# Decode attention and decode state reads as fp32 matmuls on four 32-column tiles, state loads on POOL's queue

## The chip, the core and the metric

The kernel runs on one core of one Trainium2 chip. TensorE (PE in the profile) multiplies, VectorE (DVE) and ScalarE (ACT) do elementwise work and empty PSUM, GpSimd (POOL) and SyncE (SP) issue transfers. The metric is the device time of one execution in microseconds.

## What is computed

The reference is one decoder layer for a prompt of 256 tokens and eight sequences that decode one token each. One input, two mixers in parallel, gates and an output projection:

```python
# A: sparse attention, 8 query heads on 2 key heads, head size 128
o_cmp, o_slc, o_win = nsa_sample(q, kv_cmp, kv_slc, kv_win, cache_cmp, cache_slc, st_win, page_table, cw, slopes)
#   slc: q @ kg, softmax, p @ vg over 15 gathered blocks of 64 keys and the new token, per sequence
#   win: the same over 511 keys of the window state and the new token; the state is shifted by one and stored
# B: gated delta rule, 8 heads, one 128 x 128 state per head and decoding sequence
#   o = S q, v_new = beta (v - S k), S = decay S + v_new k^T
```

The change concerns the decode side of `slc`, `win` and B. The prompt's attention and its chunked delta rule (which ends in a state `S` that is stored) lie beside it.

## The kernel before

Nearly all work of PE is the projections: 256 prompt tokens and 8 decode tokens are the 264 moving columns, and every weight tile of 128 by 1024 fp32 (512 KB, `raw`) is split into two fp32r halves, `hi` on ACT and `lo` on DVE, of which three products are accumulated in tile `acc`. Such a weight tile is 24 matmuls and is called a half here. There are 7536 `acc` matmuls.

Everything else is written as generators (`g_dec_slc`, `g_dec_win`, `g_attn`, `g_gdn`, `g_gdn_dec` and others) that advance by one `yield` per 12 `acc` matmuls (`tick`). A string `ORDER` sets which projection comes when. From what the generators emit, the Tile framework's scheduler makes a fixed order for PE, ACT and DVE; SP and POOL keep the order in which the code issues. Each engine takes its instructions strictly in that order. SP issues the weight loads; `raw`, `hi` and `lo` have three buffers each. Large tiles (`wk`, `gk`, `gv`, `sst` and their fp32r copies) share one pool of 13 slots through `slot`.

Decode attention. `gather` (L898) fetches 15 blocks for one sequence and both key heads: `gk` keys, `gv` values, two indirect transfers of POOL each, one sequence ahead. Keys are transposed by PE (`gtr`) and copied as fp32r pair into `gkx`. `qk` multiplies them by the query, which is a zero-padded fp32r pair `qm`: 128 rows hold `hi` and `lo` of all 64 query rows, so each sequence and key head adds into one PSUM tile (`gsc` for slc, `wsc` for win): per 480 or 512 keys one matmul of 128 columns and one of 64. `split1` (L801 on ACT, L802 on DVE) makes the pairs of the window keys (`wkx`), the values (`gvx`, `wvx`); `pt_split` transposes the probabilities (`ptr`) and splits them. `pv_part` multiplies them with the values (`pvo`, 256 columns), and `pv_take` (L797) adds the rows of one sequence to `acc2` on DVE. `smo` transposes `acc2` at the end.

Delta rule. `g_gdn` inverts the prompt's triangular matrices (`inv`, through `lanes`, `td`, `U` and `prod`, which go through memory on POOL's queue), then runs the chunks (`uw`, `dS`, `vn`, `og`), stores `S` with POOL's last transfer `o_S<-prod` (L1341) and transposes the output (`ogt`). `g_gdn_dec` takes the decode states two sequences at a time (1 MB, tile `sst`): load on SP (L1423), 16 fp32 matmuls that hold a head's state as weights and move 64 columns of `wq` (`sw`), three small DVE operations for `dvn` and `dod`, scaling of 16 state tiles by the decay on ACT (L1448), a rank-one update from a broadcast transpose (`vnb`, L1449) and a store on ACT's queue. `inv`, `uw`, `dS`, `vn`, `og`, `sw`, `vnb` run in PSUM tiles of one pool of two buffers. The gates Z of these outputs (`zt`, `oh`, `ol`) are projected in the same stretch; `zt` is the first reader that frees an `acc` tile there.

Of the kernel before, what the change touches and what calls it, by code (L numbers as in the profile page):

```python
# [10 lines left out]
F32 = mybir.dt.float32  # L11
# [37 lines left out]

def shape_constants():  # L50
# [12 lines left out]
    for t in range(2):  # L63
# [8 lines left out]
    row = np.arange(64)  # L72
    srow = slope[(row // 32) * 4 + row % 4]
    c.add("c64", srow[:, None] * np.arange(64)[None])
    c.add("wrow", srow[:, None] * (np.arange(8) * 64 - 512)[None])
    c.add("e64", (row[None] // 4) == np.arange(16)[:, None])
    c.add("sel", ((row[None, None] // 32) == np.arange(2)[None, :, None])
          & (((row[None, None] // 4) % 8) == np.arange(8)[:, None, None]))
    c.add("rmask", ((p[:, None] % 64) // 4) == np.arange(16)[None])
# [57 lines left out]
def program(tc, A):  # L137
# [94 lines left out]
    grow = cp.tile([64, 2], F32, name="grow")  # L232
# [260 lines left out]
    def g_qstat(h):  # L493
# [7 lines left out]
        if h == 7:  # L501
# [88 lines left out]
    def g_small(ps):  # L590
# [38 lines left out]
    def g_dec_cmp():  # L629
# [95 lines left out]
    def new_token(w):  # L725
        yield from wait("q")
        pr = tp.tile([128, 64], F32, name="ntp", tag="a", bufs=NA)
        V.tensor_tensor(pr.rearrange("p (g b r) -> p g b r", g=2, b=NB), qd,
                        knT[:, w, :, :, None].to_broadcast([128, 2, NB, 4]), ALU.mult)
        yield 3  # L730
        pt = psb("ntk")
        mm(pt[0:64, 128:129], pr, ones[:, 0:1])
        for g in range(2):
            mm(pt[0:64, 0:128], C("sel", 8)[:, 64 * g:64 * g + 64], L["kvd"][:, w, 1, g, :], start=g == 0, stop=g == 1)
        sn = tp.tile([64, 8], F32, name="ntm", tag=f"ntm{w}")
        ve = tp.tile([64, 128], F32, name="ntv", tag=f"ntv{w}")
        V.tensor_scalar(sn[:, 0:1], pt[0:64, 128:129], SCALE, None, ALU.mult)
        S.activation(ve, pt[0:64, 0:128], AF.Copy)
        L["nt", w] = sn, ve
        mark(("nt", w))  # L740

    def row_softmax(sc, n, w):
# [11 lines left out]
        V.scalar_tensor_tensor(acc2[0:64], ve, sn[:, 4:5], acc2[0:64], ALU.mult, ALU.add)  # L754

    def scores(out, sc, bias, shape):
        lo = slot("slo", [64, 960])
        lo = lo[:, 0:math.prod(shape)]
        for k, ps in enumerate(out):
            n = math.prod(shape) // len(out)  # L760
            S.activation(lo[:, n * k:n * k + n], ps[64:128, 0:n], AF.Copy, scale=SCALE)
            V.scalar_tensor_tensor(sc[:, n * k:n * k + n], ps[0:64, 0:n], SCALE, lo[:, n * k:n * k + n], ALU.mult, ALU.add)
        V.tensor_add(sc, sc, bias)
# [11 lines left out]
    def pt_split(name, sc, nt, np_):  # L775
        pt = psb("ptr")
        for t in range(nt):
            tr(pt[0:np_, 64 * t:64 * t + 64], sc[:, np_ * t:np_ * t + np_])
        P_ = slot(name, [128, 8, 128], F32R)
        v = pt[0:np_, 0:64 * nt].rearrange("p (t c) -> p t c", t=nt)  # L780
        S.activation(P_[0:np_, 0:nt, 0:64], v, AF.Copy)
        V.tensor_sub(P_[0:np_, 0:nt, 64:128], v, P_[0:np_, 0:nt, 0:64])
        return P_

    def pv_part(po, P_, np_, ts, nt, hi, lo):
        for t in ts:
            h = lambda: mm(po[:, 0:256], P_[0:np_, t, :], hi(t), start=t == 0, stop=t == nt - 1)
            if t == 0:
                h()
            mm(po[0:64, 0:256], P_[0:np_, t, 0:64], lo(t), start=False, stop=False)  # L790
            if t:
                h()

    def pv_take(po, b):
        for g in range(2):
            i = 8 * g + b
            V.scalar_tensor_tensor(acc2, po[:, 128 * g:128 * g + 128], C("rmask")[:, i:i + 1], acc2, ALU.mult, ALU.add)  # L797

    def split1(name, src, shape, np_=128):
        x = slot(name, [128, 2] + shape, F32R)  # L800
        S.activation(x[0:np_, 0], src, AF.Copy)  # L801
        V.tensor_sub(x[0:np_, 1], src, x[0:np_, 0])  # L802
        return x

    def g_dec_win():
# [30 lines left out]
        def wk_qk(b, x):  # L836
            for g in range(2):
                qk(ps, 8 * g + b, x[:, 0, g], x[:, 1, g], b + g == 0, b * g == 7)

        prev = None  # L840
        for b in range(NB):
            if b % 2 == 0:
                if b < 6:
                    load_k(b // 2 + 1)
                else:
                    load_v(0)
            x = split1("wkx", kr[b // 2][:, b % 2, :, 0:512], [2, 512])
            if prev is not None:
                yield 3
                wk_qk(b - 1, prev)  # L850
            prev = x
        yield 2
        wk_qk(7, prev)
        bb = slot("wb", [64, 2, 512])
        V.tensor_tensor(bb[:, 0].rearrange("p (n m) -> p n m", m=64), C("wrow", 64)[:, :, None].to_broadcast([64, 8, 64]),
                        C("c64", 64)[:, None, :].to_broadcast([64, 8, 64]), ALU.add)
        sc = bb[:, 1]
        yield 7
        scores([ps], sc, bb[:, 0], [512])
# [3 lines left out]
        P_ = pt_split("wP", sc, 4, 128)  # L863
        def wv_pv(b, x):
            po = PV("pvo")
            pv_part(po, P_, 128, range(4), 4, lambda t: x[:, 0, t], lambda t: x[:, 1, t])
            pv_take(po, b)

        prev = None
        for b in range(NB):  # L870
            if b % 2 == 0 and b < 6:
                load_v(b // 2 + 1)
            x = split1("wvx", vr[b // 2][:, b % 2], [4, 256])
            if prev is not None:
                yield
                wv_pv(b - 1, prev)
            prev = x
        yield 5
        wv_pv(7, prev)
        yield 7  # L880
        pt = psb("smo")
        yield 2
        for i in range(2):
            mm(pt[:, 0:64], acc2, ident[:, 64 * i:64 * i + 64], start=i == 0, stop=i == 1)
        V.tensor_add(oD, oD, pt[:, 0:64])
        mark("oD")

    def g_dec_slc():
        yield from wait("idx")
        yield from wait(("kv", 0), 4)  # L890
        G.memset(acc2, 0.0)
# [15 lines left out]
        def gk_qk(b, g, x):  # L907
            for half in range(2):
                o = slice(480 * half, 480 * half + 480)
                qk(ps[half], 8 * g + b, x[:, 0, o], x[:, 1, o], b + g == 0, b * g == 7)  # L910

        prev = None
        for b in range(NB):
            if b < NB - GP:
                kr[b + GP] = gather("gk", "cslk", b + GP)
            elif b - NB + GP < VP:
                vr[b - NB + GP] = gather("gv", "cslv", b - NB + GP)
            for g in range(2):
                x = slot("gkx", [128, 2, 960], F32R)
                for half in range(2):  # L920
                    pt = psb("gtr")
                    for t in range(4):
                        tr(pt[:, 120 * t:120 * t + 120], kr[b][0:120, g, 4 * half + t, :])
                    o = slice(480 * half, 480 * half + 480)
                    S.activation(x[:, 0, o], pt[:, 0:480], AF.Copy)
                    V.tensor_sub(x[:, 1, o], pt[:, 0:480], x[:, 0, o])
                    yield
                if prev:
                    gk_qk(*prev)
                prev = b, g, x  # L930
            del kr[b]
        yield 6
        gk_qk(*prev)
        bb = slot("sb", [64, 2, 960])
        V.tensor_tensor(bb[:, 0].rearrange("p (t n m) -> p t n m", t=8, n=15),
                        L["sbias"][:, None, 0:15, None].to_broadcast([64, 8, 15, 8]),
# [792 lines left out]
```

## Time and profile before

| | us |
|---|---|
| median of three runs | 1146.93 (1146.84 to 1148.42) |
| profiled execution | 1147.96 |
| its span in the trace | 1146.2 |
| PE busy | 1116.5 |
| PE loading weights (beside matmuls) | 1090.7 |
| DVE busy | 777.0 |
| ACT busy | 603.5 |
| POOL busy | 146.6 |

A matmul's row in the trace has a start and a modelled end; because matmuls are pipelined, rows overlap, and what one costs is the distance from its start to the next one's start. An fp32 matmul (not fp32r) has two rows. A granted clock of 1.00 is 2.4 GHz, 0.50 is 1.2 GHz.

### The profile page before, as it was taken

To read this page: it belongs to the slowest core of one execution; us is meant where nothing else is said; L and a number is where in the kernel's file an instruction comes from. 1 tells how busy PE (TensorE), PEld (TensorE's weight loads), DVE (VectorE), ACT (ScalarE), POOL (GpSimd) and SP (SyncE) were. 2 spreads that over 40 slices of the span, in tenths; PEclk is the share of its full clock that TensorE was granted. 3 is DMA by queue.
4 is the path that set the end of the run, shared out by engine and by line. 5 is a ranking of instruction groups with operands and counts; after the bars stand their busy time and mean duration, and the time that the engine had idled before them with its cause. 6 is when DMAs were issued, how large, how long until landed. Compare 5 with 4: busy or idle time off the path is not lost.

```text
span 1146.2 us, 24552 instructions
## 1 busy us (share of the span) xinstructions
PE 1116.5 (97%) x9088; PEld 1090.7 (95%) x9088; DVE 777.0 (68%) x1619; ACT 603.5 (53%) x1165; POOL 146.6 (13%) x218
## 2 busy tenths in 40 slices
PE   4999999999999999999899999999999999999998
PEld 4989999999999998998899999999999999999998
DVE  3587665444667886996888977699746685567543
ACT  4455655445635776785566644444344844454332
POOL 4430344200001311114110300100100000000000
PEclk9999999999999999999999999999999999999999
DMA  8874676335536775467996944655752555555673
GB/s 299 256 233 142 195 216 205 124 111 165 169 121 197 210 203 154 127 190 191 261 356 240 330 152 163 180 181 175 214 179 108 212 186 183 185 179 204 213 238 128
DMA packets 76842, 222.74 MB, mean 194 GB/s; under 512 B 10465, under 2 KB 27370, under 8 KB 75186
## 3 DMA queue, kind: packets, MB, share of 16 engines
q1 hardware_dynamic: 59922, 168.55, 45.5%
q0 software_dynamic: 14784, 45.61, 14.0%
q10 hardware_dynamic: 2016, 7.01, 1.6%
q8 instruction: 71, 1.16, 0.4%
q14 instruction: 49, 0.40, 0.1%
HBM read 203.14 MB, written 17.99 MB: 193 GB/s over the span
## 4 chain that ended last, share of the span: by engine, by line
PE 85%; DVE 4%; DMA 3%; issue 1%; ACT 1%; POOL 0%; ACTq 0%; POOLq 0%; DVEq 0%
PE acc L197 70%; DMA gv<-cslv,idx 2%; DVE lo L325 1%; PE po L197 1%; PE gsc L197 1%; PE gtr L194 1%; DVE lanes L1227 1%; PE ps L197 1%; PE sw L197 1%; DMA raw<-win 1%; PE inv L197 1%; PE cf L197 1%; DVE prod L1226 1%; PE pvo L197 1%; PE uw L197 1%
## 5 line engine op out<-in xcount | busy, mean ns | idle before, releaser
L324 ACT ACTIVATE hi<-raw 128x1024 fp32r<-128x1024 f32 (+1 forms) x250 | 264.1, 1056 | 328.4 <-PE acc L197 265.4
L197 PE MATMUL acc<-xh,hi 128*128 128x264 f32 (+1 forms) x1488 | 428.9, 288 | 0.3 <-ACT gate L1491 0.3
L197 PE MATMUL acc<-xl,hi 128*128 128x264 f32 (+1 forms) x1488 | 426.8, 287 | 0.0
L197 PE MATMUL acc<-xh,lo 128*128 128x264 f32 (+1 forms) x1488 | 425.6, 286 | 0.0
L325 DVE TENSOR_TENSOR lo<-raw,hi 128x1024 fp32r<-128x1024 f32 (+1 forms) x250 | 304.3, 1218 | 171.5 <-ACT hi L324 168.7
L197 PEld LDWEIGHTS acc<-xl,hi 128*128 128x128 f32 (+1 forms) x1488 | 280.6, 189 | 2.0 <-issue 0.6
L197 PEld LDWEIGHTS acc<-xh,hi 128*128 128x128 f32 (+1 forms) x1488 | 280.5, 189 | 2.0 <-ACT gate L1491 0.6
L197 PEld LDWEIGHTS acc<-xh,lo 128*128 128x128 f32 (+1 forms) x1488 | 279.6, 188 | 1.7 <-issue 0.5
L197 PE MATMUL acc<-hi,w1h 128*128 128x254 f32 (+1 forms) x512 | 147.7, 289 | 15.9 <-ACT hi L401 15.9
L197 PE MATMUL acc<-lo,w1h 128*128 128x254 f32 (+1 forms) x512 | 146.5, 286 | 3.3 <-DVE lo L402 3.1
L197 PE MATMUL acc<-hi,w1l 128*128 128x254 f32 (+1 forms) x512 | 145.1, 283 | 0.0
L402 DVE TENSOR_TENSOR lo<-rawc,hi 128x512 fp32r<-128x512 f32 (+2 forms) x136 | 84.1, 656 | 52.1 <-ACT hi L401 45.9
L197 PEld LDWEIGHTS acc<-hi,w1h 128*128 128x128 f32 x512 | 97.9, 191 | 16.0 <-ACT hi L401 15.9
L401 ACT ACTIVATE hi<-rawc 128x512 fp32r<-128x512 f32 (+2 forms) x136 | 74.7, 599 | 61.3 <-PE acc L197 56.5
L197 PEld LDWEIGHTS acc<-lo,w1h 128*128 128x128 f32 x512 | 98.6, 192 | 4.5 <-DVE lo L402 4.3
L197 PEld LDWEIGHTS acc<-hi,w1l 128*128 128x128 f32 x512 | 98.3, 192 | 0.1
L378 POOL DMA_DIRECT2D rawc<-ccmp x125 | 67.4, 539 | 97.7 <-issue 72.6
L197 PE MATMUL acc<-oh,hi 128*128 128x264 f32 x256 | 73.6, 287 | 0.2 <-ACT gate L1491 0.2
L197 PE MATMUL acc<-ol,hi 128*128 128x264 f32 x256 | 73.5, 287 | 0.0
L197 PE MATMUL acc<-oh,lo 128*128 128x264 f32 x256 | 73.4, 287 | 0.0
L197 PE MATMUL acc<-mh,hi 128*128 128x264 f32 x256 | 72.7, 284 | 0.0
L197 PE MATMUL acc<-ml,hi 128*128 128x264 f32 x256 | 72.6, 283 | 0.0
(453 smaller groups left out, 1651.9 us busy)
## 6 DMA issues: line engine op xcount, KB each, us to landing
raw<-win SPq DMA_DIRECT2D x184, 512.0 KB, 3.7
raw<-wpab SPq DMA_DIRECT2D x32, 512.0 KB, 3.3
raw<-wo SPq DMA_DIRECT2D x32, 512.0 KB, 3.5
rawc<-ccmp SPq DMA_DIRECT2D x126, 128.0 KB, 3.1
rawc<-ccmp POOLq DMA_DIRECT2D x125, 128.0 KB, 3.3
raw<-w SPq DMA_DIRECT2D x8, 512.0 KB, 5.4
wk<-winK SPq DMA_DIRECT2D x8, 512.0 KB, 9.3
o_wk<-wk POOLq DMA_DIRECT2D x8, 512.0 KB, 8.0
```

The costliest lines, as they stand in the source:

```text
L194: T.transpose(out, in_, ident[0:n, 0:n])
L197: T.matmul(out, lhsT, rhs, start=start, stop=stop, **k)
L324: S.activation(self.hi, self.raw, AF.Copy)
L325: V.tensor_sub(self.lo, self.raw, self.hi)
L378: e.dma_start(rawc[kv, b][j // 8][:, j % 8].rearrange("p s c g -> p (s c g)"), src[kv, bass.ds(r, 1)].rearrange("o d f -> (o d) f"))
L401: S.activation(h, src, AF.Copy)
L402: V.tensor_sub(l, src, h)
L1226: V.tensor_tensor(pp, Lt[:, 0:i, 0:i], La[:, i, 0:i, None].to_broadcast([64, i, i]), ALU.mult)
L1227: V.tensor_reduce(Lt[:, i, 0:i], pp.rearrange("p j c -> p c j"), AX.X, ALU.add, negate=True)
```

## The change

- The decode query stays fp32. It is laid out in `qm` as four column tiles: sequence parity and key head choose the 32-column tile, the sequence pair chooses four of 16 used columns (the rest is zero). `qk` issues four matmuls with 32 columns each, at columns 0, 32, 64 and 96 of the array, per sequence pair and 480 or 512 keys. No pair of fp32r copies is made of keys, values or probabilities; `split1`, `slo` and the masks `rmask` are gone.
- Transposed keys are copied half by ACT and half by DVE. Scores, softmax and new-token terms have 128 rows instead of 64. `pt_rows` transposes 128 rows.
- `pv_part` holds 32 columns of the probabilities as weights and moves 128 value columns, on four column tiles (key head and parity of the key block); four sequences fill one PSUM tile, which one ACT copy (`pv_take`) moves to `X`. `smo` gathers: 17 matmuls instead of 2.
- State reads: `wq` (zero-padded to 80) is the weights, the state is moved: 16 fp32 matmuls of 32 columns per sequence pair, then two ACT copies (`swr`), four transposes (`swt`) and three DVE operations for both sequences.
- `sst` is loaded by POOL's queue instead of SP's.
- Some `yield` counts are smaller, so that each sequence pair of the window branch takes 36 `acc` matmuls where it took 72.

```diff
-            SP.dma_start(ss, A["stS"][b0 // 2])
+            G.dma_start(ss, A["stS"][b0 // 2])
             yield
             yield 7
+            p3 = PGD("sw")
             for b in range(2):
-                p3 = PGD("sw")
-                bb = b0 + b
                 for h in range(8):
-                    c = h // 4 * 32
-                    mm(p3[:, 64 * h:64 * h + 64], ss[:, b, h, :], wq[:, c:c + 32, :].rearrange("p c w -> p (c w)"))
...
+                    j, c, o = h % 4, 8 * h + b0 + b, 128 * (2 * b + h // 4)
+                    mm(p3[32 * j:32 * j + 32, o:o + 128], wq[:, c:c + 16, :].rearrange("p c w -> p (c w)"), ss[:, b, h, :])
+            rows = [tp.tile([128, 256], F32, name="swr", tag="a", bufs=NA) for _ in range(2)]
+            for b in range(2):
+                S.activation(rows[b], p3[:, 256 * b:256 * b + 256], AF.Copy)
+            yield 2
+            p5 = PGD("swt")
+            for i in range(4):
+                tr(p5[:, 128 * i:128 * i + 128], rows[i // 2][:, 128 * (i % 2):128 * (i % 2) + 128])
...
-    def qk(ps, i, hi, lo, first, last):
-        qm = L["qm"]
-        a, b = qm[:, 128 * i:128 * i + 128], qm[:, 128 * i:128 * i + 64]
-        n = hi.shape[-1]
-        if first:
-            mm(ps[:, 0:n], a, hi, start=True, stop=False)
-        mm(ps[0:64, 0:n], b, lo, start=False, stop=False)
-        if not first:
-            mm(ps[:, 0:n], a, hi, start=False, stop=last)
+    def qk(ps, i, keys):
+        for j in range(4):
+            x = keys(j // 2, j % 2)
+            mm(ps[32 * j:32 * j + 32, 0:x.shape[-1]], L["qm"][:, j, i, :], x, start=i == 0, stop=i == 3)
...
-    def pv_part(po, P_, np_, ts, nt, hi, lo):
+    def pv_part(po, P_, np_, b, ts, nt, val):
+        o = 128 * (b % 4)
         for t in ts:
-            h = lambda: mm(po[:, 0:256], P_[0:np_, t, :], hi(t), start=t == 0, stop=t == nt - 1)
...
+            for g in range(2):
+                j, c = 2 * g + t % 2, 2 * (b % 2) + g
+                mm(po[32 * j:32 * j + 32, o:o + 128], P_[0:np_, t, 32 * c:32 * c + 32], val(g, t), start=t < 2, stop=t >= nt - 2)
...
-            x = split1("wkx", kr[b // 2][:, b % 2, :, 0:512], [2, 512])
...
+            yield 3
+            qk(ps, bp, lambda bl, g: kr[bp][:, bl, g, 0:512])
```

What this does to the order, at three places. On PE in the window branch, before (`wkx` is the split key pair, `qm` the query, `acc` the projections between):

```order
L197 MATMUL acc<-xh,lo 128x264
L197 MATMUL wsc<-wkx,qm 128x512
L197 MATMUL wsc<-wkx,qm 64x512 x2
L197 MATMUL wsc<-wkx,qm 128x512
L197 MATMUL acc<-xh,hi 128x264
```

and now (`wk` is the key tile as loaded):

```order
L205 MATMUL acc<-xl,hi 128x264
L205 MATMUL acc<-xh,lo 128x264
L205 MATMUL wsc<-wk,qm 32x512 x4
L205 MATMUL acc<-xh,hi 128x264
L205 MATMUL acc<-xl,hi 128x264
```

Four 32-row results stand directly behind each other; the runs of `gsc`, `pvo` and `sw` are of 4 to 16 such matmuls.

On POOL, the end of its order before (`td`, `U` and `prod` belong to the inversion, `o_S` is the store of the prompt's final state):

```order
L1238 DMA U<-td 32x16x32
L1241 DMA prod<-td 32x16x32
L1238 DMA U<-td 32x16x32 x2
L1241 DMA prod<-td 32x16x32
L1238 DMA U<-td 32x16x32
L1341 DMA o_S<-prod 128x1024
```

and now (`sst<-stS` is the load of two sequences' states):

```order
L1215 DMA U<-td 32x16x32 x2
L1218 DMA prod<-td 32x16x32
L1215 DMA U<-td 32x16x32
L1401 DMA sst<-stS 128x2048 x2
L1318 DMA o_S<-prod 128x1024
L1401 DMA sst<-stS 128x2048 x2
```

Two state loads stand ahead of the store `o_S`, two behind it. Before, the four stood in SP's order between weight loads.

On PE, behind the chunks of the prompt's delta rule, before (the last reads of a state, `sw`, with projections between them):

```order
L197 MATMUL og<-vbt,aT 128x128
L194 MATMUL vnb<-cst,dvn 128x128 x4
L197 MATMUL sw<-wq,sst 128x64 x8
L197 MATMUL acc<-xl,hi 128x264
...
L197 MATMUL acc<-xh,hi 128x264
L197 MATMUL sw<-wq,sst 128x64 x8
L194 MATMUL vnb<-cst,dvn 128x128 x4
L197 MATMUL acc<-xl,hi 128x264
```

and now (`ogt` transposes the prompt's output, `swt` the state reads; the `acc` row is the first since the second `sw`):

```order
L205 MATMUL og<-vbt,aT 128x128
L205 MATMUL sw<-sst,wq 32x128 x16
L202 MATMUL ogt<-cst,oG 128x128 x8
L202 MATMUL swt<-cst,swr 128x128 x4
L202 MATMUL ogt<-cst,oG 128x128 x4
L202 MATMUL vnb<-cst,dvn 128x128 x4
L202 MATMUL ogt<-cst,oG 128x128 x4
L202 MATMUL vnb<-cst,dvn 128x128 x12
L205 MATMUL sw<-sst,wq 32x128 x16
L202 MATMUL swt<-cst,swr 128x128 x4
L202 MATMUL vnb<-cst,dvn 128x128 x12
L205 MATMUL acc<-xh,hi 128x264
```

Between the 5568th and the 5569th `acc` matmul PE now has 24 `uw`, the second pair's `sw` and `swt`, all `dS` (16), `vn` (8) and `og` (24), 16 `vnb` and the rows above. Before, 170 `acc` matmuls (5568 to 5738) lay between the same groups. That 5569th matmul waits for DVE's `zt`, whose ACT part stands behind the scaling of the last state in ACT's order:

```order
L1432 ACTIVATE sst<-sst,deb 128x128 x15
L1411 ACTIVATE swr<-sw 128x256 x2
L1432 ACTIVATE sst<-sst,deb 128x128
L1337 ACTIVATE oB<-ogt,prm 128x2x256 x4
L1432 ACTIVATE sst<-sst,deb 128x128 x9
L1436 DMA o_Ss<-sst 128x2048
L1411 ACTIVATE swr<-sw 128x256 x2
L1432 ACTIVATE sst<-sst,deb 128x128 x7
L1460 ACTIVATE zt<-acc 128x264 x2
```

The first fifteen scalings and the copies `swr` belong to the third state pair, the nine and seven to the fourth; `zt` is last.

## Rows read from the trace of the kernel before

**Rows 1.** page, part 4: the chain that ended last, by engine and line.

```profile
PE 85%; DVE 4%; DMA 3%; issue 1%; ACT 1%; POOL 0%; ACTq 0%; POOLq 0%; DVEq 0%
PE acc L197 70%; DMA gv<-cslv,idx 2%; DVE lo L325 1%; PE po L197 1%; PE gsc L197 1%; PE gtr L194 1%; DVE lanes L1227 1%; PE ps L197 1%; PE sw L197 1%; DMA raw<-win 1%; PE inv L197 1%; PE cf L197 1%; DVE prod L1226 1%; PE pvo L197 1%; PE uw 
```

**Rows 2.** waits of PE: what it waited for, us in total, times, longest.

```profile
PE cvt L197 <- ACT qsq L1117: 1.7, 1, 1.7
PE pvo L197 <- DVE acc L797: 1.6, 1, 1.6
```

**Rows 3.** timeline of PE, selected branch: start us, us, line, form, count.

```profile
400.23 0.68 PE L197 MATMUL gsc<-gkx,qm 128*64 128x480 f32 x2
400.75 0.29 PE L197 MATMUL acc<-xl,hi 128*128 128x264 f32 x1
```

**Rows 4.** timeline of PE, selected branch, values: the same columns.

```profile
531.50 1.01 PE L197 MATMUL pvo<-gvx,sP 120*64 120x256 f32 x7
532.35 0.29 PE L197 MATMUL acc<-xl,hi 128*128 128x264 f32 x1
```

**Rows 5.** timeline of PE, window branch, scores: the same columns.

```profile
599.38 2.03 PE L197 MATMUL wsc<-wkx,qm 128*64 128x512 f32 x8
601.25 0.28 PE L197 MATMUL acc<-xh,hi 128*128 128x264 f32 x1
```

**Rows 6.** timeline of PE, delta rule: one state read between projection matmuls.

```profile
911.49 0.28 PE L197 MATMUL acc<-xh,hi 128*128 128x264 f32 x1
911.61 1.89 PE L197 MATMUL sw<-wq,sst 128*128 128x64 f32 x16
913.34 0.60 PE L194 MATMUL vnb<-cst,dvn 128*128 128x128 f32 x4
```

**Rows 7.** timeline of PE: full-array fp32 matmuls with 512 columns.

```profile
447.71 0.59 PE L197 MATMUL po<-PTt,vcp 15*128 15x512 f32 x1
...
526.26 3.70 PE L197 MATMUL po<-PTt,kTa 128*128 128x512 f32 x8
```

**Rows 8.** timeline of PE: fp32 matmuls on 32-square tiles (0, 0) and (64, 64).

```profile
835.15 0.44 PE L197 MATMUL inv<-P,prod 32*32 32x32 f32 x16
835.52 0.66 PE L197 MATMUL inv<-U,At 128*128 128x64 f32 x4
```

**Rows 9.** windows: us, busy time and instructions by engine, granted clock, DMA share, GB/s.

```profile
503.00:562.00 59.00, 55.00 (x407) 48.89 (x405) 43.38 (x79) 36.97 (x58) 14.11 (x12) 1.00 0.74 186
562.00:661.00 99.00, 98.05 (x769) 95.50 (x770) 85.47 (x180) 62.08 (x105) 19.83 (x28) 0.98 0.87 309
570.00:580.00 10.00, 10.00 (x78) 9.45 (x76) 8.99 (x16) 6.55 (x9) 1.35 (x2) 1.00 1.03 416
869.60:923.40 53.80, 53.76 (x468) 53.48 (x467) 37.04 (x122) 34.47 (x116) 0.58 (x1) 1.00 0.44 158
563.30:566.70 3.40, 3.40 (x17) 3.40 (x17) 3.12 (x8) 2.73 (x3) 1.47 (x2) 0.50 1.00 351
```

**Rows 10.** the same window, instructions on tile acc alone.

```profile
869.60:923.40 53.80, 23.52 (x172) 21.27 (x171) 1.69 (x4) 1.92 (x5) 0.00 (x0) 1.00 0.44 158
```

**Rows 11.** timeline of POOL: the last transfers that it issues.

```profile
824.06 0.65 POOL L1238 DMA_DIRECT2D U<-td  x1
908.06 0.58 POOL L1341 DMA_DIRECT2D o_S<-prod  x1 [83.35 <-DVE prod L1335]
```

**Rows 12.** tile sst: issues of its loads, first and last start; time to landing.

```profile
L1423 SPq DMA_DIRECT2D sst<-stS x4: 328/328/426, 775.2 to 882.3; - x4
...
DMA to landing us min/median/max: 4.6/5.6/7.7
```

**Rows 13.** timeline of ACT: scaling of one state.

```profile
875.35 2.44 ACT L1448 ACTIVATE sst<-sst,deb 128x128 f32<-128x128 f32 x8
```

**Rows 14.** timeline of DVE, delta rule of the prompt.

```profile
887.55 0.69 DVE L1331 COPY prod<-dS 128x512 f32<-128x512 f32 x1 [1.27 <-PE dS L197]
...
906.65 1.12 DVE L1335 SCALAR_TENSOR_TENSOR prod<-prod,edl,dS 128x128 f32<-128x128 f32 x4
```

More of the change, by code (lines that the diff above doesn't have):

```diff
@@ L231, in program @@
     gd = cp.tile([128, 64], F32, name="gd")
-    grow = cp.tile([64, 2], F32, name="grow")
+    grow = cp.tile([128, 2], F32, name="grow")
     acc2 = cp.tile([128, 128], F32, name="acc2")
@@ L785, in pv_part, with scores @@
-    def pv_part(po, P_, np_, ts, nt, hi, lo):
+        if w:
+            V.scalar_tensor_tensor(acc2, ve, sn[:, 4:5], acc2, ALU.mult, ALU.add)
+        else:
+            V.tensor_scalar(acc2, ve, sn[:, 4:5], None, ALU.mult)
+    def scores(out, sc, bias):
+        n = sc.shape[-1] // len(out)
+        for k, ps in enumerate(out):
+            V.scalar_tensor_tensor(sc[:, n * k:n * k + n], ps[:, 0:n], SCALE, bias[:, n * k:n * k + n], ALU.mult, ALU.add)
+    def qk(ps, i, keys):
+        for j in range(4):
+            x = keys(j // 2, j % 2)
+            mm(ps[32 * j:32 * j + 32, 0:x.shape[-1]], L["qm"][:, j, i, :], x, start=i == 0, stop=i == 3)
@@ L835, in g_dec_win @@
         yield 3
[L836 to L846, printed above, removed]
-            x = split1("wkx", kr[b // 2][:, b % 2, :, 0:512], [2, 512])
[L848 to L856, printed above, removed]
+        for bp in range(4):
+            if bp < 3:
+                load_k(bp + 1)
+            else:
+                load_v(0)
+            yield 3
+            qk(ps, bp, lambda bl, g: kr[bp][:, bl, g, 0:512])
+        bb = slot("wb", [128, 2, 512])
+        V.tensor_tensor(bb[:, 0].rearrange("p (n m) -> p n m", m=64), C("wrow")[:, :, None].to_broadcast([128, 8, 64]),
+                        C("c64")[:, None, :].to_broadcast([128, 8, 64]), ALU.add)
         sc = bb[:, 1]
         yield 7
-        scores([ps], sc, bb[:, 0], [512])
+        scores([ps], sc, bb[:, 0])
         yield
@@ L862, in g_dec_win @@
         yield 4
[L863 to L869, printed above, removed]
+        P_ = pt_rows("wP", sc, 4, 128)
+        L["X", 1] = slot("X1", [128, NB, 128])
         for b in range(NB):
@@ L872, in g_dec_win @@
                 load_v(b // 2 + 1)
[L873 to L877, printed above, removed]
+            if b % 4 == 0:
+                po = PV("pvo")
+            yield
+            pv_part(po, P_, 128, b, range(4), 4, lambda g, t: vr[b // 2][:, b % 2, t, 128 * g:128 * g + 128])
+            pv_take(po, 1, b)
         yield 5
-        wv_pv(7, prev)
-        yield 7
         pt = psb("smo")
-        yield 2
-        for i in range(2):
-            mm(pt[:, 0:64], acc2, ident[:, 64 * i:64 * i + 64], start=i == 0, stop=i == 1)
+        o = pt[:, 0:64].rearrange("p (g b r) -> p g b r", g=2, b=NB)
+        gx = C("gath").rearrange("p (g b r) -> p g b r", g=2, b=NB)
+        mm(pt[:, 0:64], acc2, C("perm"), start=True, stop=False)
+        for w in range(2):
+            for b in range(NB):
+                mm(o[:, :, b, :], L["X", w][:, b, :], gx[:, :, b, :], start=False, stop=w * b == 7)
         V.tensor_add(oD, oD, pt[:, 0:64])
+        del L["X", 0], L["X", 1]
         mark("oD")
@@ L906, in g_dec_slc @@
         yield 20
[L907 to L912, printed above, removed]
+        kt = {}
         for b in range(NB):
@@ L943, in g_dec_slc @@
         yield 4
[L944 removed]
+        P_ = pt_rows("sP", sc, 8, 120)
+        L["X", 0] = slot("X0", [128, NB, 128])
         yield 2
[L946 to L956 removed]
         for b in range(NB):
@@ L959, in g_dec_slc @@
                 vr[v] = gather("gv", "cslv", v)
+            if b % 4 == 0:
+                po = PV("pvo")
             for half in range(2):
-                x = split1("gvx", vr[b][0:120, :, 4 * half:4 * half + 4, :], [2, 4, 128], 120)
-                if prev:
-                    yield
-                    gv_pv(*prev)
-                prev = b, half, x
+                yield
+                pv_part(po, P_, 120, b, range(4 * half, 4 * half + 4), 8, lambda g, t: vr[b][0:120, g, t, :])
+            pv_take(po, 0, b)
             vr[b] = None
         yield
-        gv_pv(*prev)
         mark("slc")
```

173 lines of the change are left out of this document (82 added, 91 removed).

## Prediction

> **What bounds the kernel now.** I read the page's chain first: PE carries 85% of it, the `acc` matmuls alone 70% [rows 1]. The table says the same: 1116.5 of 1146.2 us busy. So a saving counts only if PE issues less or waits less, and work taken from ACT and DVE counts only where PE waits for them; around the decode attention's values these are 1.7 and 1.6 us [rows 2]. Then the timelines of PE for what each old and new form costs from start to start, the windows for DMA and clock, and POOL, ACT and DVE around the last state reads, since there the order changes most. About 0.2% (2.3 us) is what a measurement of this kernel can tell from no change. The sum is made on the profiled execution (1147.96); the median is 1.03 lower.
>
> **Prices.** An `acc` matmul takes 0.12 us [rows 6]. A `gsc` matmul takes (400.75 - 400.23)/2 = 0.26 [rows 3], a `pvo` 0.85/7 = 0.121 [rows 4], a `wsc` 1.87/8 = 0.234 [rows 5]. An fp32 matmul has two rows; a row with 64 moving columns and 128 weight columns takes 1.73/16 = 0.108 [rows 6], one with 512 columns (3.70 - 0.59)/7 = 0.44 [rows 7], so 0.41 with 480, 0.11 with 128 and 0.0275 with 32.
>
> Do four column tiles run beside each other? No row of before has column tiles that share rows. The nearest has two tiles with different rows and columns: 16 rows with 32 columns, 0.44 us if one followed the other, are done 0.37 us after the first start with the switch back to the full array in it (about 0.1) [rows 8]; so two at a time. Bounds are one at a time and four; I take four, as nothing in that row shows one tile holding up the other.
>
> **Part by part, on PE.**
> - Scores, selected branch: 64 x 0.26 = 16.6 out; 32 fp32 matmuls in, 32 x 2 x 0.41 = 26.2 in a row, 6.6 in fours: -10.0.
> - Values, selected: 128 x 0.121 = 15.5 out; 128 x 2 x 0.108 = 27.6, 6.9 in fours: -8.6.
> - Values, window: 7.7 out; 13.8, 3.5 in fours: -4.2.
> - Scores, window: 32 x 0.234 = 7.5 out; 16 x 2 x 0.44 = 14.1, 3.5 in fours: -4.0.
> - First state read: 3.5 out; 0.9 in fours and four transposes of 0.11 in: -2.2. The other three belong to the stretch below.
> - `smo`: 17 x 2 x 0.108 = 3.7 for 0.4: +3.3.
> - Some 45 runs change the array's layout and back: between nothing (the change from 128 to 64 columns leaves `wsc` at 0.234) and 0.2 each as in [rows 8]: +0 to +9, I take +2.
>
> Together -23.7. In a row these fp32 matmuls would take 26.2 + 27.6 + 13.8 + 14.1 + 3.5 = 85.2, in fours 21.3.
>
> The splits that vanish from ACT and DVE, and the transposed keys that they now share, gain only in the two waits: 3.3 us, and 3.4 us at half clock behind the first (17 starts in 3.4 us where 0.12 each would be 2.0: 1.4) [rows 2, 9]. Values still come by the same gathers, one sequence ahead, so I credit -2 of -4.7. Elsewhere this relief is worth nothing.
>
> DMA: from 503 to 562 us the queues had share 0.74, 44 us of 59 [rows 9]. Now PE's work there shrinks to 59 - 4 - 8.6, about 47, and window keys come into it (4 MB, 10 us at the 416 GB/s of the fullest row): 54 in 47. From 562 to 661 it was 99 us x 309 GB/s = 30.6 MB; now 408 instead of 584 `acc` matmuls pass, 176/24 x 0.52 = 3.8 MB less in weights, for about 73 us: 367 GB/s, under 416. So 0 to 7 from the first, 0 to some 5 from unevenness: +4.
>
> **The stretch behind the 5568th `acc` matmul.** Two edits meet there. POOL keeps its order, so state loads three and four now wait behind `o_S`, which waited for DVE's last `prod` until 908.06 [rows 11]; SP had issued the last load at 882.3 [rows 12]. Behind these loads PE's `sw` waits, behind it every `acc`, since PE's order has none until the fourth state is through; and that one waits for `zt`, which ACT has behind the last scalings. Counted from the 5568th matmul:
> 1. 24 `uw` are 24 x 0.215 = 5.2, `sw` 0.9; ACT's 14 scalings, (2.44 - 0.40)/7 = 0.29 each [rows 13], 4.1, stand between copies that PE needs; `dS` starts at about 11.
> 2. 48 fp32 matmuls (`dS`, `vn`, `og`) 10.3, 16 transposes 1.7, and DVE between them four times 0.69 and once 1.12 [rows 14]: 16, of which some 2 overlap. `S` is final at 25.
> 3. `o_S` 0.6, issue 0.6, landing 5.6 [rows 11, 12]: 32.
> 4. Third pair: `sw` 0.9, 15 scalings 4.4 ahead of the copies 0.8, `swt` 0.4, `dvn` 0.5, three groups of `vnb` paced by four updates like the 1.12 of [rows 14] 3.5: 42.5.
> 5. Fourth: `sw` 0.9, nine scalings 2.6, copies 0.8, seven scalings 2.0, `zt` 0.4 and its DVE half 0.4: 50.
>
> Before, the same work lay in 53.8 us without idle time, of which 172 x 0.121 = 20.8 were `acc` [rows 9, 10]: 33.0. The 16 `ogt` now inside (1.7) came later before. So 50 - 33.0 - 1.7 = +15 at full clock. But PE now waits 1 to 7 us at a time, and behind a wait of 1.7 us the granted clock was 0.50, 1.2 GHz [rows 2, 9]. PE's steps above are some 22 us; at half clock all through they would cost 22 more, never 0. I take 9, as waits are thickest in the later half. Together +24, bounds +9 (step 1 and 2 shorter by 6, no clock loss) and +37.
>
> The first state load also moves, behind `U` and `prod`: 824.06 + 0.65 + 5.6 is 830, and PE reaches that part of the inversion at 835 [rows 8, 11, 12]; that cover of 5 us gone, each microsecond later is one of PE's.
>
> **Sum.** -23.7 - 2 + 4 + 24 = +2.3; 1147.96 + 2.3 - 1.03 = 1149.
>
> The Trainium skill, TensorE: Matmul & The Clock Gate, Part 3 (Measured speedup vs the span model), gives 2.38x for three column tiles of 32 with 512 columns, not 3x. No run here shows it. By an estimate from that page, four would give 3.2x, these matmuls 26.9 instead of 21.3, and the sum 1155.
>
> **Rivals.**
> - *The stretch stays short, the savings hold.* Same sum with the stretch at +12, layout +1, DMA +1, the old waits -3: -25.7 + 1 + 1 - 3 + 12 = -14.7, 1132. For it: my chain adds steps as if none overlapped, and the old order had PE busy all through. Against it: the order has no `acc` in between, and the landing time alone is 5.6.
> - *Slower: weight loads of column tiles don't hide.* The 256 fp32 matmuls need 512 loads of 32 columns; hidden they cost nothing. Not hidden, by the 0.0275 that 32 columns take, 512 x 0.0275 = 14: 1163. It decides slower from 0.2 us on. Against it: `acc` matmuls follow at 0.12, 264 columns take 0.11 at full clock, and their loads of 128 columns find no room but beside the matmul before [rows 6]. For it: short matmuls (0.11) leave less cover. The same page, in Part 3 (The mechanism), says that a weight load overlaps running matmuls only where its row group differs; all four column tiles share theirs. The trace disagrees for the full array.
> - *The change does not do what it says: column tiles run two at a time, or one.* Then they take 42.6 or 85.2 instead of 21.3: 1170 or 1213. [rows 8] shows two at a time and cannot show four.
>
> **How the numbers follow.** Chances: forecast 0.45 (1142 to 1158), short stretch 0.30 (1122 to 1142), loads that don't hide 0.12 (1158 to 1168), two or one at a time 0.13. Faster by over 0.2% (under 1144.6): 0.30 and 0.08 of the forecast's 0.45, 0.38. Within 0.2%: 0.14 of it. Slower: its other 0.23 and 0.25, 0.48. The range 1130 to 1171 leaves out about 0.09 below, the lower third of the short stretch, and 0.09 above, one at a time and half of two.
>
> **What would show it.** `gsc` in fours at about 0.83 us per four matmuls and `wsc` at 0.9; 0.9 us for eight `pvo`, 1.8 if two at a time. In the stretch: two state loads issued right behind `o_S`, some 6 us without PE work behind it, about 50 us from the 5568th to the 5569th `acc`, and a granted clock of 0.5 in places. I am wrong if that distance is under 42 us, if `gsc` fours take 1.6 us, or if PE waits over 10 us for weights or gathers between 500 and 660 us.

## The result and the profile after

The changed kernel takes 1161.38 us (median of four runs, 1159.74 to 1162.99), the kernel before 1147.68 in the same comparison: ratio 1.0115, 95% interval 1.0092 to 1.0139. It is slower by 13.7 us. The profiled executions have spans of 1158.1 and 1146.2.

Page, parts 1 and 4 (busy time by engine; the chain that ended last by engine, then by line):

```profile
PE 1113.8 (96%) x9334; PEld 1064.9 (92%) x9334; DVE 725.6 (63%) x1538; ACT 571.4 (49%) x1126; POOL 142.0 (12%) x221
...
PE 76%; issue 11%; DVE 4%; DMA 4%; SPq 2%; ACT 1%; POOL 1%; POOLq 1%; ACTq 0%; DVEq 0%
```

DVE lost 51 us of work and ACT 32, but PE, which carried 85% of the chain [rows 1], is busy only 2.7 us less. PE now waits for what it did not wait for before; of the waits of [rows 2] none is left (waits of PE, us in total, times, longest):

```profile
PE sw L205 <- DMA sst<-stS: 7.5, 1, 7.5
PE swt L202 <- ACT swr L1411: 7.2, 4, 2.4
PE inv L205 <- DMA U<-td: 1.1, 1, 1.1
```

The `acc` matmuls stand in nearly the same sequence in every kernel here (at most 144 of the 7536 in another place, all between the 3579th and the 5858th), so their numbers serve as a clock: the start of the 2000th, 5550th and 6000th cut out the attention with the inversion (piece 1) and the end of the delta rule (piece 2). From 6000 on all kernels here run alike; ahead of the 2000th, where nothing differs, the profiled executions differ by up to 7 us, which the pieces leave out.

| | piece 1 | piece 2 |
|---|---|---|
| before | 589.1 | 91.4 |
| after | 581.5 | 110.9 |
| after minus before | -7.6 | +19.5 |

So there was a gain in piece 1, smaller than forecast, and a loss in piece 2, which is larger.

**The column tiles.** Timeline of PE, a run of `wsc` and of `pvo` between projections (start, us, line, form, count):

```profile
565.09 0.28 PE L205 MATMUL acc<-xl,hi 128*128 128x264 f32 x1
565.21 0.28 PE L205 MATMUL acc<-xh,lo 128*128 128x264 f32 x1
565.42 1.07 PE L205 MATMUL wsc<-wk,qm 128*32 128x512 f32 x8
566.42 0.39 PE L205 MATMUL acc<-xh,hi 128*128 128x264 f32 x1
566.65 0.28 PE L205 MATMUL acc<-xl,hi 128*128 128x264 f32 x1
566.77 0.28 PE L205 MATMUL acc<-xh,lo 128*128 128x264 f32 x1
...
510.94 0.28 PE L205 MATMUL acc<-xh,lo 128*128 128x264 f32 x1
511.15 0.64 PE L205 MATMUL pvo<-gv,sP 120*32 120x128 f32 x16
511.72 0.55 PE L202 MATMUL pst<-cst,zz 128*128 128x128 f32 x3
```

Eight rows with 512 columns take 1.00 us, where [rows 7] gave 0.44 for one: they run four at a time. The single records start at 565.424, .431, .438 and .444, and the next four from 565.878 on. The 16 rows of `pvo` take 0.57. But at the edges more is paid than before. From the last `acc` to the run it is 0.21 where one `acc` follows another in 0.12; the last round takes 0.52 instead of 0.43; the first `acc` behind it takes 0.23 instead of 0.12. Together 0.09 + 0.09 + 0.11 = 0.29 us for each run that leaves the full array and comes back; with the whole run instead of its last round (1.00 - 2 x 0.43 = 0.14) it is 0.34. The loader's own timeline shows why (its rows lead the matmuls):

```profile
565.09 0.19 PEld L205 LDWEIGHTS acc<-xh,lo 128*128 128x128 f32 x1
565.42 0.16 PEld L205 LDWEIGHTS wsc<-wk,qm 128*32 128x32 f32 x8
566.42 0.19 PEld L205 LDWEIGHTS acc<-xh,hi 128*128 128x128 f32 x1 [0.84 <-issue]
566.53 0.19 PEld L205 LDWEIGHTS acc<-xl,hi 128*128 128x128 f32 x1
```

Among `acc` matmuls, and within the run, the next weights are loaded a round ahead. Across a change of layout the load starts only with the matmul that needs it, at 565.42 and 566.42.

It is not the number format: `uw` is fp32 too, but on the full array, and its eight rows and the first `acc` behind them take 859.12 - 858.11 = 1.01 us, which is 8 x 0.111 and 0.12 (timeline of PE, the changed kernel):

```profile
857.99 0.29 PE L205 MATMUL acc<-xh,hi 128*128 128x264 f32 x1
858.11 0.39 PE L205 MATMUL uw<-vbt,U 128*128 128x128 f32 x2
...
858.92 0.37 PE L205 MATMUL acc<-xl,hi 128*128 128x264 f32 x1
859.12 0.28 PE L205 MATMUL acc<-xh,lo 128*128 128x264 f32 x1
```

**The stretch behind the 5568th `acc`.** That matmul starts at 861.83, the next one at 914.45, 52.6 us later. Timelines of POOL and PE (in brackets the idle time before and what ended it):

```profile
887.37 0.54 POOL L1318 DMA_DIRECT2D o_S<-prod  x1 [43.95 <-DVE prod L1312]
887.91 1.12 POOL L1401 DMA_DIRECT2D sst<-stS  x2
```

```profile
872.91 1.06 PE L205 MATMUL dS<-vbt,ktk 128*128 128x128 f32 x8
...
894.41 1.94 PE L205 MATMUL sw<-sst,wq 128*32 128x128 f32 x32 [7.50 <-DMA sst<-stS]
...
899.89 0.70 PE L202 MATMUL swt<-cst,swr 128*128 128x128 f32 x4 [2.05 <-ACT swr L1411]
...
906.80 1.08 PE L205 MATMUL sw<-sst,wq 128*32 128x128 f32 x32 [0.38 <-DVE sst L1433]
910.30 0.71 PE L202 MATMUL swt<-cst,swr 128*128 128x128 f32 x4 [2.42 <-ACT swr L1411]
...
914.45 0.57 PE L205 MATMUL acc<-xh,hi 128*128 128x264 f32 x1
```

The same stretch as windows (busy time by engine, granted clock, DMA share, GB/s); before, its work lay beside 172 `acc` matmuls at clock 1.00 [rows 9, 10]:

```profile
861.83:914.45 52.62, 34.57 (x316) 30.35 (x314) 28.18 (x96) 32.81 (x117) 1.59 (x3) 0.87 0.28 107
887.00:895.00 8.00, 0.59 (x12) 0.56 (x16) 4.53 (x15) 2.58 (x12) 1.59 (x3) 0.72 0.79 291
895.00:905.00 10.00, 7.45 (x60) 6.18 (x52) 2.10 (x9) 7.84 (x22) 0.00 (x0) 0.71 0.07 29
905.00:916.00 11.00, 6.73 (x59) 5.52 (x60) 6.84 (x27) 6.01 (x21) 0.00 (x0) 0.77 0.25 98
```

### The profile page after: what moved, and what is told of

It reads as the page before. It is cut to its first block, busy times and chain, and to the rows that moved or that the text cites. A ratio compares the mean times of both kernels' runs of the same rounds, so it can differ in the third digit from the quotient of the medians.

```text
span 1158.1 us, 24872 instructions
## 1 busy us (share of the span) xinstructions
PE 1113.8 (96%) x9334; PEld 1064.9 (92%) x9334; DVE 725.6 (63%) x1538; ACT 571.4 (49%) x1126; POOL 142.0 (12%) x221
## 4 chain that ended last, share of the span: by engine, by line
PE 76%; issue 11%; DVE 4%; DMA 4%; SPq 2%; ACT 1%; POOL 1%; POOLq 1%; ACTq 0%; DVEq 0%
PE acc L205 64%; DVE lanes L1204 1%; PE po L205 1%; PE pvo L205 1%; DVE lo L333 1%; PE gtr L202 1%; DMA raw<-w 1%; PE ps L205 1%; PE gsc L205 1%; DMA rawc<-ccmp 1%; SPq L385 1%; SPq L386 1%; POOLq L385 1%; DMA o_wk<-wk 1%; ACT sst L1432 1%
## 5 line engine op out<-in xcount | busy, mean ns | idle before, releaser
L205 PE MATMUL acc<-xh,hi 128*128 128x264 f32 (+1 forms) x1488 | 434.0, 292 | 1.0 <-ACT hi L332 1.0
```

The source lines that it names most:

```text
L205: T.matmul(out, lhsT, rhs, start=start, stop=stop, **k)
```

## The experiments

Two theories on the stretch. **A**: the order of PE has no `acc` there because of buffers. `zt`, the first reader that frees an `acc` tile, takes its tile from the same five rotating buffers (tag `a`) as the new `swr`; the first `zt` needs the buffer of the third pair's `swr`, so no `acc` may start until that pair has been read. **B**: the cost is POOL's order, with the last two loads behind `o_S`. The table has every run; pieces as above, from the profiled execution. The medians are from several comparisons, in which the kernel before took 1147.68 to 1149.53. Three kernels that are alike in piece 1 agree there within 0.2 us, but the times of one kernel spread by 3 to 13 us, so a step of 2 or 3 us in one piece proves little.

| kernel | median us | ratio to before, 95% | piece 1 | piece 2 |
|---|---|---|---|---|
| after, loads on SP | 1162.11 | 1.0114 (1.0091 to 1.0137) | 595.5 | 97.0 |
| after, own `swr` buffers | 1146.80 | 0.9969 (0.9950 to 0.9988) | 581.7 | 97.0 |
| both | 1155.47 | 1.0048 (1.0025 to 1.0070) | 595.7 | 88.7 |
| own buffers, `o_S` last | 1141.51 | 0.9943 (0.9920 to 0.9966) | 581.6 | 91.3 |
| and value runs of 16 | 1139.99 | 0.9928 (0.9905 to 0.9951) | 577.1 | 91.3 |
| and value runs of 32 | 1136.59 | 0.9907 (0.9887 to 0.9928) | 576.4 | 92.4 |
| and whole score runs | 1136.61 | 0.9914 (0.9888 to 0.9940) | 579.0 | 90.7 |
| before, loads on POOL | 1156.43 | 1.0050 (1.0024 to 1.0077) | 592.0 | 97.9 |
| attention alone, loads on SP | 1153.45 | 1.0036 (1.0023 to 1.0050) | 597.5 | 89.3 |
| attention alone, loads on POOL | 1148.31 | 1.0014 (0.9989 to 1.0040) | 584.5 | 94.8 |
| delta rule alone, as changed | 1168.87 | 1.0179 (1.0156 to 1.0202) | 584.9 | 114.9 |
| delta rule alone, own buffers | 1157.81 | 1.0068 (1.0041 to 1.0094) | 586.5 | 102.7 |

**Loads back on SP (after, one line).**

```diff
-            G.dma_start(ss, A["stS"][b0 // 2])
+            SP.dma_start(ss, A["stS"][b0 // 2])
```

> The changed kernel with one line undone: the state loads go back to SP's queue. Theory A (the empty stretch behind the 5568th acc matmul comes from zt and swr sharing one rotating set of five buffers: the zt that frees an acc tile takes the buffer of the third pair's swr, so no acc can start before that pair's swt): the stretch stays empty of acc, only the 7.5 us wait for the third load goes, so about 1152 (1148 to 1156). Theory B (the stretch comes from the loads standing behind o_S on POOL): the stretch goes, about 1142 (1138 to 1145).

Measured 1162.11: neither time. Piece 2 is shorter by 13.9, more than the 7.5 of A, but the stretch stays empty of `acc`, as A says and B does not: from the 5568th to the 5569th are 37.3 us, with the reads of three pairs in them (timeline of PE):

```profile
877.06 0.37 PE L205 MATMUL acc<-xh,lo 128*128 128x264 f32 x1
...
906.52 1.08 PE L205 MATMUL sw<-sst,wq 128*32 128x128 f32 x32 [1.41 <-DVE sst L1433]
...
914.38 0.57 PE L205 MATMUL acc<-xh,hi 128*128 128x264 f32 x1
```

And piece 1 is longer by 14. In the changed kernel the large tiles come round in another order, and the first load now needs the slot of `lanes`, which is free only when `td` has been stored. SP waits for it with the weight loads behind it (timeline of SP, its waits, then windows):

```profile
783.02 5.95 SPq L327 DMA_DIRECT2D raw<-win  x3
808.15 0.33 SPq L1401 DMA_DIRECT2D sst<-stS  x1
808.57 0.38 SPq L327 DMA_DIRECT2D raw<-win  x1
```

```profile
SPq L1401 <- DMA td<-lanes: 19.0, 2, 17.7
```

```profile
802.00:810.00 8.00, 1.62 (x14) 1.41 (x12) 2.17 (x2) 0.00 (x0) 2.85 (x5) 0.86 0.40 85
810.00:820.00 10.00, 3.86 (x39) 3.01 (x40) 1.23 (x1) 5.93 (x18) 2.50 (x4) 0.50 1.03 290
```

PE works 1.62 of 8 us, and then at the lower clock. On POOL the load stands behind `td`, so nothing else waits with it.

**Own buffers for `swr` (after, loads on POOL as changed).**

```diff
-            rows = [tp.tile([128, 256], F32, name="swr", tag="a", bufs=NA) for _ in range(2)]
-            for b in range(2):
-                S.activation(rows[b], p3[:, 256 * b:256 * b + 256], AF.Copy)
+            rows = [acc2] + [tp.tile([128, 128], F32, name="swr", tag=k) for k in ("swr", "ntv0", "ntv1")]
+            for b in range(4):
+                S.activation(rows[b], p3[:, 128 * b:128 * b + 128], AF.Copy)
```

> The changed kernel, loads still on POOL behind o_S, but the four row copies swr lie in buffers of their own (128 columns each) instead of the five that zt, kbe and others rotate through. Theory A: acc matmuls come back between the state steps, the stretch costs no more than before, about 1142 (1138 to 1146). Theory B: the third and fourth pair still wait behind o_S, at best the wait is filled, 1152 to 1161.

Measured 1146.80, 14.6 less than the changed kernel (16.2 by each one's difference to before), with piece 2 at 97.0. The loads still stand behind `o_S` (POOL), and PE no longer waits for them; its two longest waits in piece 2 are these (second fence, waits of PE):

```profile
901.08 0.54 POOL L1318 DMA_DIRECT2D o_S<-prod  x1 [55.71 <-DVE prod L1312]
901.62 1.12 POOL L1401 DMA_DIRECT2D sst<-stS  x2
```

```profile
PE swt L202 <- ACT acc L1411: 3.1, 1, 3.1
PE acc L205 <- DVE zt L1461: 1.6, 1, 1.6
```

From the 5568th to the 5569th `acc` are now 5.5 us. So the shared buffers are what takes the `acc` out of PE's order; the order of the queue, the same in both, stops PE only where no `acc` is left to fill the time. The edit also makes four copies out of two, which no run separates from the change of buffers.

**Both edits.**

> Both edits: loads on SP and swr in buffers of its own. Theory A: hardly other than own buffers alone, within 3 us of it, about 1141. Theory B: as with the loads on SP alone, 1142. If layout changes of the array cost 0.29 us for each of some 45 runs, the savings outside the stretch stay at 8 to 10 us, not the 22 forecast, so it can't reach 1130.

Measured 1155.47, not 1141 or 1142. Piece 1 pays the wait for `lanes` again. Each edit alone takes some 14 us out of piece 2, both together 22.2 (to 88.7): with `acc` free to run, the queue's order still costs 8.3.

**`o_S` issued last, own buffers.**

```diff
-        G.dma_start(A["o_S"], Sg)
+        L["Sg"] = Sg
...
+        G.dma_start(A["o_S"], L["Sg"])
```

> The version with own buffers for swr, and in addition o_S issued by POOL behind the four state loads instead of ahead of the last two. Theory A (the rows that zt and swr shared were what held the fifth acc group back, and with them apart the queue's order is covered): POOL still waits for the last prod of DVE at o_S, some 44 us, and the third and fourth pair's loads stand behind it, but acc work now fills PE, so moving o_S gives nothing: 1147, within 2 us of the version with own buffers alone. Theory B (loads behind o_S still cost: the two pairs' sw come at the 5780th and 5900th acc, and what hangs on them ends late): the pairs come some 120 acc earlier, which takes back the 2 to 5 us that PE still waits in swt, zt and vnb of the stretch: 1142 to 1145.

Measured 1141.51, 5.3 under own buffers alone (4.5 by each one's difference to before), and piece 2 is 5.6 shorter: here B holds. PE's waits in piece 2 fall by only 2.2, from 6.6 to 4.4; the mean granted clock there rises from 0.93 to 0.98, as the 12.3 us without `acc` around the fourth pair (from 931.0) are gone. The last load is issued at 877.30 and `o_S` behind it:

```profile
877.30 0.53 POOL L1401 DMA_DIRECT2D sst<-stS  x1 [15.72 <-DVE dod L1419]
902.81 0.54 POOL L1437 DMA_DIRECT2D o_S<-prod  x1 [24.98 <-DVE prod L1312]
```

**Larger runs of values (on that version).** Window values, two sequences (or four) in one run; the selected ones in the same way:

```diff
-            yield
-            pv_part(po, P_, 128, b, range(4), 4, lambda g, t: vr[b // 2][:, b % 2, t, 128 * g:128 * g + 128])
-            pv_take(po, 1, b)
+            if b % 2:
+                yield 2
+                for c in (b - 1, b):
+                    pv_part(po, P_, 128, c, range(4), 4, lambda g, t: vr[c // 2][:, c % 2, t, 128 * g:128 * g + 128])
+                    pv_take(po, 1, c)
```

> The same as the run with o_S last, and the values' products taken together: one run of 16 pvo per sequence and piece instead of two of 8, and the window values of two sequences in one run; some 15 changes between column tiles and full-width matmuls fewer, the number of matmuls as it was. Theory L (each change there and back costs 0.285 us, read from the trace of the changed kernel): 4.3 us less than the run with o_S last. Theory M (the 0.285 belongs to the matmuls or to the acc around them, not to the change): no difference. In either theory up to 2 us may be lost if the larger runs wait for their gathers, which the waits of pvo would show.

> Larger runs again: the values of two sequences in one run of 32 pvo, the window values of four in one. Some 20 changes fewer than the run with o_S last. Theory L: 5.7 us less than that run, 1.4 less than the runs of 16. Theory M: no difference from either. If PE waits at the larger runs (pvo behind GpSimd's or the queue's gathers, or acc behind the softmax's rows that stand later), the waits name it and the gain shrinks by their sum.

Measured 1139.99 and 1136.59. I had counted the runs wrongly: the scheduler had already joined some, and `pvo` goes from 29 runs to 19 and 14, so 10 and 15 fewer, not 15 and 20. At 0.29 that is 2.9 and 4.4; piece 1 is shorter by 4.6 and 5.2. Of the medians' steps, the 1.5 lies within the spread of the runs and the 4.9 does not (1134.68 to 1138.87 against 1139.35 to 1144.25). So the sign is Theory L's, and the price per run is confirmed only roughly. One of the joined runs, timeline of PE; 64 rows in 1.88, with one change there and back:

```profile
529.71 0.28 PE L205 MATMUL acc<-xh,lo 128*128 128x264 f32 x1
529.92 1.96 PE L205 MATMUL pvo<-gv,sP 120*32 120x128 f32 x64
531.80 0.61 PE L205 MATMUL cvt<-cst,qsq 128*128 128x1 f32 x4
```

**Whole runs of scores.** One `yield` more ahead of the selected scores (on runs of 32):

```diff
-                yield 2
+                yield 3
```

> The version with the larger value runs, and one `yield` more ahead of the selected scores, so that the key copies of both heads are there and the eight gsc of a sequence pair stand in one run. In the changed kernel and in the version with larger runs these 32 matmuls stand in 8 runs (6, 1, 1, 2, 6, 6, 2 and 8 matmuls), which makes 24 rounds of rows where 16 full ones would do. Theory R (a round with one or two of the four column tiles used takes as long as a full one, 0.41 us, and each run costs its 0.285): 8 rounds are 3.3 us and 3 runs 0.9, so 4 us less than the version with larger runs, 1131 to 1134 against a before of 1148.5. Theory S (a round costs by the tiles in it, so that splitting costs nothing but the change): about 1 us less, 1135 to 1137. The four runs of gsc in the trace, 16 rows each, should last four rounds, 1.7 us.

In the changed kernel the eight matmuls of one sequence pair were split, here six, one and one, and rounds ran with one or two tiles. Now those of three pairs stand together and the last pair's in seven and one (timelines of PE, the changed kernel and this version):

```profile
399.78 1.80 PE L205 MATMUL gsc<-gkx,qm 128*32 128x480 f32 x12
401.51 0.55 PE L202 MATMUL pst<-cst,zz 128*128 128x128 f32 x3
402.00 0.99 PE L205 MATMUL gsc<-gkx,qm 128*32 128x480 f32 x2
```

```profile
424.35 1.82 PE L205 MATMUL gsc<-gkx,qm 128*32 128x480 f32 x16
426.10 0.63 PE L202 MATMUL gtr<-cst,gk 120*128 120x120 f32 x4
```

Twelve rows took 1.73 us, two took 0.92, four elsewhere 0.93, sixteen take 1.75. A round is paid by its columns, not by the tiles in it; all `gsc` together fall from 10.66 to 7.91 us. That is Theory R at the place. But the kernel is no faster (1136.61): the order behind it is another, and PE waits 2.4 us longer in piece 1, part of it for `U`.

**The parts alone.** The queue first, in the kernel before:

> The kernel before with nothing changed but the queue of the four state loads, POOL in place of SyncE. Theory A (the queue alone costs nothing as long as acc may fill PE while the third and fourth load stand behind o_S): 1146 to 1150. Theory B (the queue's order is the cost in itself): the third pair comes some 40 us later and PE waits for it: 1155 to 1165.

Measured 1156.43, slower by 6.9: B's number, though not by B's wait. Both pieces are longer (+2.9 and +6.5), but PE does not wait for the load; the last state reads start up to 941.5 instead of 913.2 and PE waits 3.9 for `zt` behind them. The attention alone, with the old delta rule:

> The changed decode attention with the delta rule of before (states as weights, loads on SP, no swr). Both theories: no empty stretch. From the two traces the attention had gained 13.3 us at the 5300th acc matmul, of which some 5.5 us were the first state's work that was only moved, so 1147.7 - 8 = 1140 (1136 to 1143). Had the attention cost time itself, it would come out at 1148 or more.

> The attention of the changed kernel with the delta rule of the kernel before, and its state loads from GpSimd's queue as in the changed kernel. Theory A (in the run with these loads on SyncE's queue, its 1153.5 came from the first load's wait for the slot of lanes, with the weight loads of the following stretch behind it on that queue): with the loads on POOL this wait is not on SyncE's queue, the low clock around 810 to 820 us goes, and what is left is the attention's own gain, 7.9 us by the acc positions of the changed kernel up to the 5550th, plus or minus 3: 1138 to 1143. Theory Q (the attention by itself brings nothing, its gain is paid back behind it whichever queue loads the states): 1148 to 1153. With the old delta rule the third load also stands behind o_S on POOL; if that decides, PE waits for sst over 6 us at the third pair.

Measured 1153.45 and 1148.31. The first has the wait for `lanes` on SP, which I had not foreseen (piece 1: 597.5); the second has not, but is Theory Q's number, not A's 1138 to 1143: the attention's 4.6 in piece 1 go to the queue's 3.4 in piece 2. With the loads on POOL the old attention is 6.9 slower than its before and the new one 0.2 faster, so the attention is worth some 7 us where the queue is the same. The delta rule alone, as changed and with own buffers:

> The attention of the kernel before with the delta rule of the change as it is in the diff: column tiles, swr in the buffers that zt uses too, loads on POOL. Theory A (the shared buffers make the changed kernel's loss, whatever the attention does): no acc can start between the 5568th and the fourth pair's reads, as in the changed kernel; what the changed kernel lost behind the 5550th acc, 19.5 us, comes whole, less about 2 us of the first pair's reads and some of the old attention's waits: 1162 to 1168. Theory Q (the loss came from the new attention's rotation of buffers): 1146 to 1150.

> The attention of the kernel before with the delta rule on column tiles and swr in buffers of its own, loads on POOL behind o_S. Theory A: the distance from the 5568th to the 5569th acc goes back to a few us and the reads are cheaper by 2 to 4 us than the old ones, of which PE waits for the late pairs take some: 1144 to 1149, some 15 to 20 under the run with the shared buffers. Theory Q: the same time as that run, within 3 us.

Measured 1168.87 and 1157.81. With the shared buffers 58.4 us without `acc` follow the 5568th, and piece 2 is 23.5 over before: the loss belongs to the delta rule, whatever the attention does. Own buffers give 11 back, not the 15 to 20 expected; what remains is near the queue's price alone (1156.43), so the state reads on column tiles bring nothing that these runs could show.

## Why the prediction was right, and where its steps were not

1149 was forecast as the likeliest, with 0.48 for slower as the likeliest sign; 1161.38 lies in the range, 12 above the number. It does not lie in the 1142 to 1158 that I gave the forecast's own mechanism, but in the 1158 to 1168 of the rival in which weight loads don't hide, which the trace refutes inside a run. So the range held partly by luck: piece 1 gained 14.1 less than forecast and the stretch lost 4.5 less. In the profiled executions the forecast sum was +2.3 and the measured one +11.9.

| term | forecast | measured |
|---|---|---|
| `gsc` | -10.0 | -5.6 |
| `pvo`, both branches | -12.8 | -8.0 |
| `wsc` | -4.0 | -2.5 |
| first state read | -2.2 | -2.0 |
| `smo` | +3.3 | +3.7 |
| layout changes, at `acc` | +2 | +5.8 |
| waits | -2 | -2.2 |
| DMA | +4 | 0 |
| all other tiles | 0 | +3.2 |
| piece 1 | -21.7 | -7.6 |
| stretch, piece 2 | +24 | +19.5 |

The measured terms are distances from start to start on PE, summed by tile over piece 1; what a distance has above 0.6 us counts as a wait (4.9 before, 2.7 now, none of them an old one). DMA stands at 0 because no wait for the gathers or the window's loads is among them.

- **Four tiles side by side, loads hidden: right.** Inside a run a round of four takes 0.43 with 512 columns and 0.11 with 128, as priced. The rivals built on the contrary (1163, and 1170 or 1213) fall. At the edges of a run, though, no load is hidden, and by the price of an edge that costs about what the first of them came to, 14. My sign of 0.9 us for eight `pvo` was twice my own price (16 rows in four rounds of 0.108 are 0.43); they take 0.57. The rule in the Trainium skill, TensorE: Matmul & The Clock Gate, Part 3 (The mechanism), that a load overlaps running matmuls only where its row group differs, does not hold here: the second round's loads start at 565.451, 0.43 ahead of their matmuls, on the same rows. (The same section also lets a load into the background weight buffer go ahead.) The 2.38x of Part 3 (Measured speedup vs the span model) is for three tiles; here the first run of `wsc`, eight rows, would take 8 x 0.434 = 3.47 alone and takes 1.00 + 0.09 + 0.11 = 1.20 with both edges, 2.9 times less, so with the edges counted the 3.2 estimated from that page was nearer than my 4.
- **The mis-sized term is the layout change.** I took +2 for some 45 runs, with +9 as the upper bound. 44 runs at 0.29 are 12.8 (at 0.34, 15.0): the edge inside the runs sits in the rows of `gsc`, `pvo` and `wsc`, the rest at `acc`. I saw one edge of about 0.1 in [rows 8]; the way in had another (from the `acc` at 834.94 to `inv` at 835.15 it is 0.21, not 0.12). I let the change from 128 to 64 columns in [rows 5] outweigh them, whose rows show no such edge. The Trainium skill, TensorEngine Tiling (Array Packing), Tiling Modes (Key Properties), states that changing the mode drains TensorE; the loader's rows above agree, as no load goes ahead of a change.
- **Rounds that are not full.** I priced `gsc` as 16 rounds; the order had it in 24, 8 x 0.41 = 3.3 too few. This could be read from the order beforehand: it has runs of one and two matmuls, where I wrote of 4 to 16. The 3.2 us of all other tiles, among them `po` (+0.8), `inv` (+0.8) and `dec` (+0.9), are not attributed.
- **DMA +4: nothing came.** From 503 to 562 us the share rose from 0.74 [rows 9] to 0.87, and PE waits for no transfer there:

```profile
503.00:562.00 59.00, 59.00 (x590) 47.74 (x589) 25.08 (x54) 24.66 (x43) 13.60 (x14) 1.00 0.87 227
```

- **The stretch, step by step: right in size.** `dS` at 11, measured 872.91 - 861.83 = 11.1; `S` final at 25, measured 25.5; third load landed at 32, 32.6; fourth pair's `sw` at 42.5, 45.0; the end at 50 and 9 for the clock, 52.6 with the clock in it. The clock cost at most 5.4 (the last two windows: 10 x 0.29 and 11 x 0.23, had PE issued in all of their low-clock time), so the 9 was too much. By my own subtraction 52.6 - 33.0 - 1.7 = 17.9 of the 19.5; the other 1.6 lie elsewhere in piece 2. The short-stretch rival (1132, with +12) fell: the wait of 7.50 for the load is there as forecast.
- **Its cause was only half named.** I listed the loads behind `o_S`, and that PE's order had no `acc`, and put the latter down to `zt` behind the scalings in ACT's order. The runs show that the order itself follows from `zt` and `swr` sharing buffers, and that either cause, taken away alone, gives 14 of piece 2 back: with the loads on SP 37.3 us without `acc` remain, with own buffers 5.5. My cover of 5 us for the moved first load held: PE waits nowhere for it.

## What to carry to other kernels

Count how often a small tiled matmul interrupts full-array work: here each return trip cost 0.29 us, and joining runs, with the matmuls as they were, gave 4.9. A new temporary tile in an old rotating tag ties its readers to all other users of that tag; look for who needs the buffer next, above all if that frees what the busiest engine fills. Before a load is moved to another queue, ask which wait for its buffer moves with it and what is queued behind: the same move, from SP to POOL, cost 7 us in the kernel before, gave 5 with the new attention alone and 9 with both parts and own buffers.

## What the runs showed of the hardware that I had not expected

Four 32-column tiles that share all rows start 7 ns apart, and so do their weight loads; a round of one or two tiles takes as long as a round of four (`gsc`: two rows 0.92 us, four 0.93, sixteen in four rounds 1.75). Between the full array and column tiles no weights are loaded ahead, in either direction, which costs 0.09, 0.09 and 0.11 us at the three edges of a run.
